# Reuse of the late spill's rows, early loads of the second convolution, and the order of the last sum

## The chip, the cores and the metric

One core of one Trainium2 chip runs one program. The metric is the time of one execution on the device in microseconds (us). TensorE (PE) multiplies, VectorE (DVE) and ScalarE (ACT) compute element by element, GpSimd (POOL) takes a few small operations, and SyncE (SP) issues most of the transfers (DMA) between the core's SBUF and the device's memory.

## The reference

One layer for two groups of tokens with the same weights: 1024 prompt tokens and 256 sample tokens of 1024 features, all in float32. The FFN is 2816 wide.

```python
def short_conv_mixer(x, w_in, conv_w, w_out):
    b, c, v = jnp.split(x @ w_in, 3, axis=-1)
    u = c * v
    up = jnp.pad(u, ((0, 0), (pad, pad), (0, 0)))
    conv = sum(up[:, j:j + S] * conv_w[j] for j in range(CONV_WIDTH))
    return (b * conv) @ w_out
...
def swiglu(x, w_in, w_out):
    gate, up = jnp.split(x @ w_in, 2, axis=-1)
    return (jax.nn.silu(gate) * up) @ w_out
...
        h = rms_norm(x, norms[i, 0])
        x = x + rms_norm(short_conv_mixer(h, ...), norms[i, 1])
        h = rms_norm(x, norms[i, 2])
        x = x + rms_norm(swiglu(h, ffn_w_in[i], ffn_w_out[i]), norms[i, 3])
```

## The kernel before

**Products.** Each float32 operand is split into a high part (rounded by ACT, `copy` L106 or `split` L93) and the rest (DVE, `sub` L97 or `split` L94). Each product is three products of parts (TERMS). Prompt tokens use a form with seven products instead of eight: x1, z5, x6, z3, y2, x7, x4. They add up in three PSUM banks x, y and z. A bank is read out between its products (by ACT's `copy` into `y` in the first group of the output product, by DVE's `add` else), and PE has to wait for that before it writes the bank again.

**Stages.** (1) Input product of the mixer: 12 units (`SEQ`), of which the last makes the last two feature blocks. (2) `store` (L418) splits the gated convolution into `zst` tiles and writes them to memory (`zd`, L424). (3) The second convolution product `mm2` (L664) works by token tile of 128 tokens: it loads `zs` (`load_z`, from `zd`), does 48 products of 128x512 into `mx`, and `after_mm2` makes the norm, the residual x1 and `ht`. `transposes` (L638) turns `ht` round with eight small PE products. `ORDER2` lists the tiles; the first two (0 and 4) run together. (4) FFN in, 22 blocks. (5) FFN out.

**Spill.** The FFN's activations are kept in memory (`actd`). `spill(j)` takes a pair j of feature blocks and makes seven parts of it (`part`). Each part takes a row tile `st{j}_c` of the pools "a" or "s", fills it with one ACT copy and one DVE subtraction, writes it with two stores of 320 KB and returns the row. The next user of the row waits on the chip for those stores to land. The last pair (10) is spilled while the output product is already running, as `st10_0` to `st10_6`; FFN out reads pair 10 in its last group.

**FFN out.** 25 units: five groups of feature pairs times five units of two token tiles (`UNITS`). A unit's data come as one `ut` (1 MB) and three small `us` (256 KB each; for x7, y2 and x4). The weights of pair j come as `w4r{j}` rows and are turned into blocks by ACT and DVE (`weights`). All of it is put in order by a planner that is written out by hand: `clock` holds its estimate of when each engine is free, `slot` (L1119) emits one product, and `advance` (L1067) emits the next background step (a weight step or a spill step) if it would end before a limit. `landing` (L892) is its estimate of when a transfer lands, and `row_free` holds the time from which a row of the pools counts as free. Order on each engine is as emitted, and each engine runs its instructions in order. Unit 4's x4 is emitted two products late, behind the next unit's z5, as for every unit.

**End.** For the last unit (token tiles 8 and 9), `norm_right` and `norm_left` make the squares and the product with the gain for the two halves of a row. `scale` (row, half) then does the last scaling and writes out; half 0 on SP's queue, half 1 on ACT's. `n3r` is the reciprocal root, made by a short DVE step and a power on POOL.

**Pools.** "b" has 23 slots of 8 KB, "a" three rows, "s" two rows.

Of the kernel before, what the change touches and what calls it, by code (L numbers as in the profile page):

```python
# [14 lines left out]
P = 128  # L15
# [21 lines left out]
def encoder_kernel(ctx: ExitStack, tc: tile.TileContext, xT, x, g0T, gB, cwT, w1, w2, w3, w4, out_p, out_s):  # L37
# [51 lines left out]
    def f32(ap):  # L89
        return ap.bitcast(F32)  # L90
# [257 lines left out]
    class EvMul:  # L348
# [69 lines left out]
        def store(self, d):  # L418

            for h in (0, 1):  # L420
                st = get(f"zst{self.e}{d}{h}", [2, HALF], F32R, kind="a")
                split(st[:, 0], st[:, 1], rows[d][:, h])
                for p in (0, 1):
                    nc.sync.dma_start(  # L424
                        zd[h, :, :, p, 2 * self.e + d].rearrange("q p t -> p q t"),
                        f32(st[:, p]).rearrange("p (q t) -> p q t", t=P),
                    )
                put(st)
# [174 lines left out]
    def w2_steps():  # L603
# [5 lines left out]
        while len(w2r) < min(len(w2t) + 3, KD) and (len(free["a"]) > 2 or len(free["b"]) > 2):  # L609
            w2r.append(get(f"w2r{len(w2r)}", [D], kind="a" if len(free["a"]) > 2 else "b"))  # L610
            nc.sync.dma_start(w2r[-1], w2[len(w2r) - 1])

    pending.append(w2_steps)
    for n in range(2, len(SEQ)):
        u = SEQ[n]
        follow = SEQ[n + 1 : n + 3] + [None, None]
        final = n == len(SEQ) - 1
        ev = EvC(u[2]) if u[1] == 1 else EvMul(u[1], u[2])
        if final:
            put(r2)  # L620
            w2_steps()
        b = Block(u, ev, *follow[:2], final)
        b.p12()
        b.p657()
        b.sample()
        b.p43()


# [4 lines left out]
        nc.sync.dma_start(gb[:, i], gB[i].partition_broadcast(P))  # L633
    ar = {(kh, c): get(f"ar{kh}{c}", [KH, 512]) for kh in (0, 1) for c in (0, 1)}
    hs[:] = [get(f"hs{p}", [KD, 256], F32R) for p in "hl"]
    hts, mx, zs = {}, {}, {}

    def transposes(i):  # L638
        for q in range(2):
# [14 lines left out]
                t0 = (i - 8) * P  # L654
                split(*(h[:, 4 * q : 4 * q + 4, t0 : t0 + P] for h in hs), ov)
        put(hts.pop(i))

    def load_z(i, k0=0, k1=KD):
        if i not in zs:
            zs[i] = get(f"zs{i}", [2, KD, P], F32R)  # L660
        src = zd[i // 4, i % 4] if i < 8 else zd[i - 8, 4]
        nc.sync.dma_start(f32(zs[i][:, :, k0:k1]), src[:, :, k0:k1])

    def mm2(*tiles, ks=range(KD)):  # L664
        for i in tiles:
# [27 lines left out]
        nc.vector.scalar_tensor_tensor(out=hts[i], in0=x1, scalar=r, in1=gb[:, 1], op0=ALU.mult, op1=ALU.mult)  # L693
        put(x1)

    ORDER2 = [i for uu in UNITS for i in uu]
    xts = {}

    def load_xt(i):
# [13 lines left out]

    F0, F1, F2 = (("f", f) for f in range(3))
    for i in ORDER2[:2]:
        load_xt(i)
        load_z(i, 0, KD - 2)
    for i in ORDER2[:2]:
        load_z(i, KD - 2, KD)
    for n, i in enumerate(ORDER2):  # L720
        last = n == NT - 1
        if n == 0:
            mm2(i, ORDER2[1])
        elif n > 1:
            if n == 8:
                load_z(ORDER2[9])
                cb["a11"] = [get(f"a11{p}", [KH, 512], F32R) for p in "hl"]
                s3 = get("s3", [KH, 512])
                early_sums(slice(0, 3 * P))
            mm2(i, ks=range(1))  # L730
            transposes(ORDER2[n - 2])
            if last:
                early_sums(slice(3 * P, 4 * P))
            mm2(i, ks=range(1, KH))
            if last:
                put(*w2t[:KH])
                make_c("a12", a12)
                add(a12, a12, a11)
                make(F0, "t24")
                make_c("s2", a11)  # L740
                put(a11)
            mm2(i, ks=range(KH, KD))
        if last:
            put(*w2t[KH:])
        after_mm2(i)
        if n and not last:
            if n != 8:
                load_z(ORDER2[n + 1])
            load_xt(ORDER2[n + 1])
        if n == 4:  # L750
            load(F0)
            for what in ("g", "u", "sums"):
                make(F0, what)
# [11 lines left out]
    def spill(j):  # L765

        a, b = act.pop(2 * j), act.pop(2 * j + 1)
        a11, a21, a12, a22 = a[:, 0], a[:, 1], b[:, 0], b[:, 1]

        def part(c, src, ready=None):  # L770
            done = yield "act", 0.75, ready, 0, 1, 0
            st = get(f"st{j}_{c}", [2, HALF], F32R, kind="as" if j == KP - 1 else "s")
            copy(st[:, 0], src)
            done = yield "dve", 0.76, done, 0, 0, 0
            sub(st[:, 1], src, f32(st[:, 0]))
            for p in range(2):
                nc.sync.dma_start(
                    actd[:, j, :, (2 * c + p) * P : (2 * c + p + 1) * P].rearrange("u p t -> p u t"),
                    f32(st[:, p]).rearrange("p (u t) -> p u t", t=P),
                )  # L780
            put(st)
            return done

        def change(op, out, x, y):
            done = yield "dve", 0.76, None, 0, 0, 0
            op(out, x, y)
            return done

        yield from part(A11, a11)
        yield from part(A12, a12)  # L790
        yield from part(A22, a22)
        done = yield from change(add, a21, a21, a22)
        yield from part(S1, a21, done)
        done = yield from change(sub, a11, a11, a21)
        yield from part(S2, a11, done)
        done = yield from change(add, a22, a22, a11)
        yield from part(S3, a22, done)
        done = yield from change(add, a12, a12, a11)
        yield from part(S4, a12, done)
        put(a, b)  # L800
        act_left.discard(j)
# [265 lines left out]
    def advance(entry, limit):  # L1067
        gen, (engine, cost, ready, places, rows, gi) = entry
        if gi > at["group"] + 1 or places and len(free["b"]) < places + keep() or rows and rows_free() < rows:
            return False  # L1070
        ready = ready() if callable(ready) else ready or 0.0
        if rows:
            tags = (free["s"] + free["a"])[:rows]
            ready = max([ready] + [row_free.get(tag, 0.0) for tag in tags])
        done = max(clock[engine], ready) + cost
        if done > limit:
            return False
        clock[engine] = done
        before = rows_free()
        try:  # L1080
            entry[1] = gen.send(done)
        except StopIteration:
            background.remove(entry)
        if rows_free() > before:
            row_free[(free["a"] + free["s"])[-1]] = done + 4.5
            for tag in free["s"][-1:] + free["a"][-1:]:
                row_free[tag] = max(row_free.get(tag, 0.0), done + 4.5)
        return True

    def fill(limit):  # L1090
# [109 lines left out]
    def norm_left(row):  # L1200
        i = UNITS[-1][row]
        r = tail["r", i]
        squares(tail["acc", i], 0, y_half(row, 0))
        mul(tail["yg", i][:, :H], y_half(row, 0), tail["g3"][:, :H])
        nc.vector.tensor_scalar(
            out=r, in0=tail["acc", i][:, 0:1], scalar1=1.0 / D, scalar2=tail["part", i],
            op0=ALU.mult, op1=ALU.add,
        )
        nc.gpsimd.tensor_tensor(out=r, in0=r, in1=nhalf[:, :1], op=ALU.pow)
# [34 lines left out]
    begin(spill(KP - 1))  # L1244
    with tc.manual_schedule():
        clock.update(pe=0.0, act=1.0, dve=2.0, dma=0.0)
        LAST = len(GROUPS) - 1
        for n, (gi, ui) in enumerate(STREAM):
            at.update(group=gi, unit=n)
            while not set(made).issuperset(GROUPS[gi]):  # L1250
                if not any(advance(entry, 1e12) for entry in list(background)):
                    raise RuntimeError("no place for the weights")
            if gi == LAST:
                load_x1(ui)
            while keep() and len(free["b"]) or rest_asked[0] == 0:
                load_units()
            if first_tiles and first_tiles[0][0] <= n:
                raise RuntimeError("no place for a unit")
            slot(n, "x1")
            slot(n, "z5")  # L1260
            if n:
                slot(n - 1, "x4")
                at["delayed"] = n - 1
                if gi == LAST and ui:
                    begin(finish(ui - 1, 1), 1 if len(background) and background[0][0] is not w4_gen else 0)
            slot(n, "x6")
            slot(n, "z3")
            if n < END:
                slot(n, "y2")
                if gi == LAST:  # L1270
                    begin(finish(ui, 0), 0)
                slot(n, "x7")
        slot(END, "x7")
        while background:
            if not any(advance(entry, 1e12) for entry in list(background)):
                raise RuntimeError("no place at the end")
        norm_right(0)
        norm_right(1)
        slot(END, "y2")
        norm_left(0)  # L1280
        scale(0, 0)
        scale(0, 1)
        slot(END, "x4")
        norm_left(1)
        scale(1, 0)
        scale(1, 1)

# [39 lines left out]
```

## Time and profile before

| what | us |
|---|---|
| median of 3 runs | 1285.08 (1282.38 to 1285.32) |
| the profiled execution | 1286.38 |
| its span, from first to last instruction | 1284.6 |
| PE busy in it | 1246.4 |
| DVE busy | 840.7 |
| ACT busy | 465.4 |

The span is what the trace covers; the 1.78 us beside it lie outside. A row of a timeline gives the start, the length, the engine, the line, the operation with its output and inputs, and the count of equal instructions. A bracket at its end gives the idle time just before it and what ended it.

### The profile page before, as it was taken

Reading aid. Unit: us, or ns where it says so; the run is one execution under the profiler, and the core shown is the slowest. Engines: PE = TensorE matmul, PEld = TensorE weight load, DVE = VectorE, ACT = ScalarE, POOL = GpSimd, SP = SyncE. Lnnn points to the kernel's source line nnn. Section 1 sums busy time; section 2 is a strip of 40 time slices with the busy share of each in tenths; the row PEclk is TensorE's granted clock in tenths of the full one; section 3 lists DMA queues with packets and bytes.
Section 4 is the critical chain, followed back from the end, with each engine's and each line's share of the span. In section 5 each row is a group of like instructions: output and inputs, shape, how many; then the busy total and the mean of one; then the engine's idle time right before and its main releaser. Section 6 shows DMA issues by size and latency. Waiting matters only on the chain.

```text
span 1284.6 us, 15904 instructions
## 1 busy us (share of the span) xinstructions
PE 1246.4 (97%) x6213; PEld 1055.6 (82%) x6213; DVE 840.7 (65%) x1177; ACT 465.4 (36%) x694; POOL 27.0 (2%) x49
## 2 busy tenths in 40 slices
PE   8799999999999989999999999999999979999997
PEld 6588888888778868888888888888888868888885
DVE  7996655748264786565664754755667458769566
ACT  7743333325133553343343333433434331112011
POOL 0100000000011100000000000000000000000000
PEclk9899999999999989999999999999999989999999
DMA  7405041224963213453552643643636789666894
GB/s 263 164 34 148 33 116 66 80 85 147 327 230 115 94 43 118 139 161 100 157 157 87 176 136 97 176 125 95 189 116 213 248 274 329 202 226 212 284 330 167
DMA packets 185595, 207.37 MB, mean 161 GB/s; under 512 B 7984, under 2 KB 145584, under 8 KB 184496
## 3 DMA queue, kind: packets, MB, share of 16 engines
q1 hardware_dynamic: 185088, 205.83, 49.5%
q8 instruction: 49, 0.80, 0.3%
q10 hardware_dynamic: 432, 0.53, 0.1%
q14 instruction: 26, 0.21, 0.1%
HBM read 134.89 MB, written 71.43 MB: 161 GB/s over the span
## 4 chain that ended last, share of the span: by engine, by line
PE 88%; DVE 6%; DMA 3%; ACT 1%; issue 1%; POOL 1%; SPq 0%; DVEq 0%; POOLq 0%; ACTq 0%
PE xo L1131 11%; PE zo L1131 6%; PE mx L672 5%; PE yo L1131 3%; DMA wrf__3029<-w 1%; PE xv__150 L204 1%; PE xf__3543 L204 1%; PE xf__6682 L204 1%; PE xf__3760 L204 1%; PE xf__7635 L204 1%; PE xf__7456 L204 1%; PE xf__7243 L204 1%; PE xf__7069 L204 1%; PE xf__6856 L204 1%; PE xf__6469 L204 1%
## 5 line engine op out<-in xcount | busy, mean ns | idle before, releaser
L672 PE MATMUL mx<-w2s,zs 128*128 128x512 f32 x480 | 111.3, 391 | 3.0 <-DMA zs<-zd 3.0
L672 PEld LDWEIGHTS mx<-w2s,zs 128*128 128x128 f32 x480 | 89.4, 188 | 21.6 <-issue 3.4
L106 ACT ACTIVATE st<-act 128x640 fp32r<-128x640 f32 x77 | 56.8, 737 | 105.2 <-DMA actd<-st 70.0
L97 DVE TENSOR_TENSOR st<-act,st 128x640 fp32r<-128x640 f32 x77 | 63.2, 821 | 28.4 <-ACT st L106 27.7
L100 DVE TENSOR_TENSOR y<-y,xo 128x512 f32<-128x512 f32 x85 | 58.2, 685 | 28.6 <-PE xo L1131 28.3
L1131 PE MATMUL xo<-w4t,us 128*128 128x512 f32 x273 | 68.9, 389 | 0.0
L1131 PE MATMUL xo<-w4t,ut 128*128 128x512 f32 x222 | 57.0, 397 | 6.5 <-ACT y L106 6.5
L1131 PEld LDWEIGHTS xo<-w4t,us 128*128 128x128 f32 x273 | 51.2, 188 | 10.7
L1131 PEld LDWEIGHTS xo<-w4t,ut 128*128 128x128 f32 x222 | 42.3, 191 | 16.0 <-ACT y L106 6.9
L106 ACT ACTIVATE w4t<-w4r 128x1024 fp32r<-128x1024 f32 (+1 forms) x23 | 23.5, 1023 | 73.1 <-DVE w4r L97 60.2
L100 DVE TENSOR_TENSOR y<-y,zo 128x512 f32<-128x512 f32 x45 | 30.8, 685 | 18.2 <-PE zo L1131 17.9
L1131 PE MATMUL zo<-w4b,ut 128*128 128x512 f32 x165 | 42.7, 398 | 0.0
L1131 PE MATMUL xo<-w4b,ut 128*128 128x512 f32 x165 | 41.6, 390 | 0.0
L1131 PE MATMUL zo<-w4t,ut 128*128 128x512 f32 x165 | 41.5, 389 | 0.0
L1163 ACT ACTIVATE junk<-y 128x1024 f32<-128x1024 f32 (+1 forms) x12 | 11.0, 917 | 75.5 <-DVE y L100 74.2
L1131 PEld LDWEIGHTS zo<-w4b,ut 128*128 128x128 f32 x165 | 31.8, 193 | 6.8
L1131 PEld LDWEIGHTS xo<-w4b,ut 128*128 128x128 f32 x165 | 31.0, 188 | 6.6
L1131 PEld LDWEIGHTS zo<-w4t,ut 128*128 128x128 f32 x165 | 31.0, 188 | 6.5
L106 ACT ACTIVATE w4b<-w4r 128x512 fp32r<-128x512 f32 (+1 forms) x22 | 18.0, 838 | 35.1 <-DMA us<-actd 16.0
L414 DVE SCALAR_TENSOR_TENSOR row<-u,cw,row 128x256 f32<-128x256 f32 (+1 forms) x32 | 28.0, 881 | 4.2 <-ACT row L412 3.9
L1131 PE MATMUL yo<-w4b,us 128*128 128x512 f32 x114 | 29.2, 392 | 0.0
L97 DVE TENSOR_TENSOR w4t<-w4r,w4t 128x1024 fp32r<-128x1024 f32 (+1 forms) x23 | 26.9, 1173 | 0.7 <-ACT w4t L106 0.7
(2120 smaller groups left out, 3359.1 us busy)
## 6 DMA issues: line engine op xcount, KB each, us to landing
actd<-st SPq DMA_DIRECT2D x154, 320.0 KB, 2.8
ut<-actd SPq DMA_DIRECT2D x20, 1024.0 KB, 6.6
us<-actd SPq DMA_DIRECT2D x62, 256.0 KB, 4.6
ut<-actd SPq DMA_DIRECT2D x16, 768.0 KB, 8.2
zd<-zst SPq DMA_DIRECT2D x32, 320.0 KB, 3.3
zs<-zd SPq DMA_DIRECT2D x8, 1024.0 KB, 6.7
w4r<-w SPq DMA_DIRECT2D x11, 512.0 KB, 4.0
w4r<-w SPq DMA_DIRECT2D x22, 256.0 KB, 4.5
```

Source lines behind the costliest of these rows:

```text
L97: nc.vector.tensor_tensor(out=out, in0=a, in1=b, op=ALU.subtract)
L100: return nc.vector.tensor_tensor(out=out, in0=a, in1=b, op=ALU.add)
L106: nc.scalar.activation(out, a, AF.Copy)
L204: nc.tensor.matmul(out[:, :n], stat(w, k), mov(part, k), start=first and k == 0 and j == 0, stop=last and k == KH - 1 and j == 2, skip_gro ...
L414: nc.vector.scalar_tensor_tensor(out=out, in0=src, scalar=cw[:, j, dd : dd + 1], in1=out, op0=ALU.mult, op1=ALU.add)
L672: nc.tensor.matmul(mx[i][h], zs[i][:, part, k], w2t[k][:, w, h * H : (h + 1) * H], start=k == 0 and j == 0, stop=k == KD - 1 and j == 2,)
L1131: nc.tensor.matmul(acc, stat[n, c, j][:, ap], w[wp], start=starts and jn == 0 and m == 0, stop=jn == len(grp) - 1 and m == 2, skip_group_c ...
L1163: nc.scalar.activation(junk, src, AF.Square, accum_out=acc[:, col : col + 1])
```

## The change

- `store`: the tiles `zst` of the last feature blocks are taken from pool "b" and no longer from "a".
- `load_z` and `ORDER2` move up. In the last unit of the input product the loads of k 0 to 5 of the first two tiles are issued behind `b.sample()`, ahead of the last two products (`p43`). What is left behind the loop are k 6 and 7.
- `mm2`: for the third and fourth tile six k (36 products) rather than one go ahead of the transposes.
- `part` of `spill`: a returned row counts as free at the planner's estimate of when the part's stores (0.625 MiB) land, plus 1.0. What `advance` noted before (the step's end plus 4.5, for the rows of both pools) goes. `row_free` is emptied at the start of the output product.
- End: `norm_left` becomes a generator that stops ahead of `n3r`. The product x4 of the last unit, with its sum into `y`, is emitted ahead of the scalings of row 0; the squares and the gain of row 1 follow, then one scaling of row 0, `n3r` of row 1, and the other three scalings.

```diff
         def store(self, d):
...
-                st = get(f"zst{self.e}{d}{h}", [2, HALF], F32R, kind="a")
+                st = get(f"zst{self.e}{d}{h}", [2, HALF], F32R, kind="a" if self.e < KH - 1 else "b")
...
         b.sample()
+        if final:
+            for i in ORDER2[:2]:
+                load_z(i, 0, KD - 2)
         b.p43()
...
     for i in ORDER2[:2]:
+        load_z(i, KD - 2, KD)
+    for i in ORDER2[:2]:
         load_xt(i)
-        load_z(i, 0, KD - 2)
-    for i in ORDER2[:2]:
-        load_z(i, KD - 2, KD)
...
-            mm2(i, ks=range(1))
+            early = KD - 2 if n < 4 else 1
+            mm2(i, ks=range(early))
             transposes(ORDER2[n - 2])
             if last:
                 early_sums(slice(3 * P, 4 * P))
-            mm2(i, ks=range(1, KH))
+            mm2(i, ks=range(early, KH))
...
-            mm2(i, ks=range(KH, KD))
+            mm2(i, ks=range(max(early, KH), KD))
...
+            row_free[held[id(st)][1]] = landing(0.625) + 1.0
             put(st)
             return done
...
         clock[engine] = done
-        before = rows_free()
         try:
             entry[1] = gen.send(done)
         except StopIteration:
             background.remove(entry)
-        if rows_free() > before:
-            row_free[(free["a"] + free["s"])[-1]] = done + 4.5
-            for tag in free["s"][-1:] + free["a"][-1:]:
-                row_free[tag] = max(row_free.get(tag, 0.0), done + 4.5)
         return True
...
         mul(tail["yg", i][:, :H], y_half(row, 0), tail["g3"][:, :H])
+        yield
         nc.vector.tensor_scalar(
...
         clock.update(pe=0.0, act=1.0, dve=2.0, dma=0.0)
+        row_free.clear()
...
         slot(END, "y2")
-        norm_left(0)
+        for _ in norm_left(0):
+            pass
+        slot(END, "x4")
+        left = norm_left(1)
+        next(left)
         scale(0, 0)
+        next(left, None)
         scale(0, 1)
-        slot(END, "x4")
-        norm_left(1)
         scale(1, 0)
         scale(1, 1)
```

SP's queue at the end of the input product, before. `zst300` to `zst311` are the tiles of the last two feature blocks, `gb` the gains, `xt` the residual's input.

```order
L633 DMA gb_2578<-gB 128x1024 x2
L424 DMA zd_106<-zst300_2544 128x5x128 x2
L662 DMA zs0_2589<-zd_106 128x2x768
L662 DMA zs4_2593<-zd_106 128x2x768
L424 DMA zd_106<-zst301_2549 128x5x128 x2
L424 DMA zd_106<-zst310_2568 128x5x128 x2
L424 DMA zd_106<-zst311_2573 128x5x128 x2
L701 DMA xt0_2587<-x 128x1024
L701 DMA xt4_2591<-x 128x1024
L662 DMA zs0_2589<-zd_106 128x2x256
L662 DMA zs4_2593<-zd_106 128x2x256
```

The same place now.

```order
L619 DMA zs4_2533<-zd_106 128x2x768
L619 DMA zs0_2531<-zd_106 128x2x768
L645 DMA gb_2582<-gB 128x1024
L424 DMA zd_106<-zst300_2548 128x5x128 x2
L424 DMA zd_106<-zst311_2577 128x5x128 x2
L645 DMA gb_2582<-gB 128x1024
L424 DMA zd_106<-zst301_2553 128x5x128 x2
L706 DMA xt0_2593<-x 128x1024
L424 DMA zd_106<-zst310_2572 128x5x128 x2
L619 DMA zs4_2533<-zd_106 128x2x256
L706 DMA xt4_2595<-x 128x1024
L619 DMA zs0_2531<-zd_106 128x2x256
```

The loads of `zs4` and `zs0` (k 0 to 5) have moved from behind `gb` and two stores to the head of the row; the loads of k 6 and 7 stay behind the stores, and two of the stores have changed places.

ACT in the last units of the first group of the output product, before. `y3` and `y4` are the outputs of units 3 and 4, `xo0_4` and `zo0_4` unit 4's banks.

```order
L106 ACTIVATE st10_1_8029<-act20_7455 128x640
L106 ACTIVATE y3_8065<-xo0_3_8056 128x512
L106 ACTIVATE y3_8065<-zo0_3_8067 128x512
L106 ACTIVATE st10_2_8081<-act20_7455 128x640
L106 ACTIVATE y2_7977<-xo0_2_7967 128x512
L106 ACTIVATE w4b11_1_7935<-w4r3_8025 128x512
L106 ACTIVATE y3_8065<-xo0_3_8056 128x512
L106 ACTIVATE w4b22_3_8108<-w4r3_8025 128x1024
L106 ACTIVATE st10_5_8139<-act21_7634 128x640
L106 ACTIVATE y4_8141<-xo0_4_8129 128x512
L106 ACTIVATE w4t13_3_8150<-w4r3_8025 128x1024
L106 ACTIVATE y4_8141<-zo0_4_8143 128x512
```

The same place now.

```order
L106 ACTIVATE y3_8059<-xo0_3_8050 128x512
L106 ACTIVATE st10_1_8068<-act20_7455 128x640
L106 ACTIVATE y3_8059<-zo0_3_8061 128x512
L106 ACTIVATE y2_7972<-xo0_2_7962 128x512
L106 ACTIVATE w4b11_1_7930<-w4r3_8019 128x512
L106 ACTIVATE y3_8059<-xo0_3_8050 128x512
L106 ACTIVATE w4b22_3_8110<-w4r3_8019 128x1024
L106 ACTIVATE y4_8132<-xo0_4_8122 128x512
L106 ACTIVATE y4_8132<-zo0_4_8134 128x512
L106 ACTIVATE w4t13_3_8149<-w4r3_8019 128x1024
L106 ACTIVATE y3_8059<-xo0_3_8050 128x512
L106 ACTIVATE y4_8132<-xo0_4_8122 128x512
```

`st10_2` and `st10_5` no longer stand among these rows: `st10_1` is the one spill copy left there, and behind `w4b22_3` come both first copies of unit 4 directly.

SP's queue at the same place, before. `ut5` and `us4` are the loads of units 5 and 4.

```order
L923 DMA w4r40_8042<-w4 128x1024
L925 DMA w4r41_8043<-w4 128x512 x2
L1007 DMA ut5_0_8063<-actd_108 128x2x1024
L1007 DMA us4_4_0_8090<-actd_108 128x2x256
L1007 DMA us4_5_0_8092<-actd_108 128x2x256
L1007 DMA us4_6_0_8094<-actd_108 128x2x256
L777 DMA actd_108<-st10_2_8081 128x5x128 x2
L1007 DMA ut6_0_8136<-actd_108 128x2x1024
L777 DMA actd_108<-st10_5_8139 128x5x128 x2
```

The same place now.

```order
L929 DMA w4r40_8036<-w4 128x1024
L931 DMA w4r41_8037<-w4 128x512 x2
L1013 DMA ut5_0_8057<-actd_108 128x2x1024
L782 DMA actd_108<-st10_1_8068 128x5x128 x2
L1013 DMA us4_4_0_8088<-actd_108 128x2x256
L1013 DMA us4_5_0_8090<-actd_108 128x2x256
L1013 DMA us4_6_0_8092<-actd_108 128x2x256
L1013 DMA ut6_0_8129<-actd_108 128x2x1024
L1013 DMA us5_4_2_8160<-actd_108 128x2x256
L1013 DMA us5_5_2_8162<-actd_108 128x2x256
L1013 DMA us5_6_2_8164<-actd_108 128x2x256
L782 DMA actd_108<-st10_2_8185 128x5x128 x2
```

Two stores (`st10_1`) stand ahead of the three `us4` where before two (`st10_2`) stood behind them, and `us5` follows `ut6` directly.

DVE at the end, before. `xo4_4` is the bank of the last product x4; rows 8 and 9 are the last unit's two token tiles.

```order
L100 TENSOR_TENSOR y4_8141<-y4_8141,yo4_4_9748 128x512
L103 TENSOR_TENSOR yg8_9735<-y4_8141,g3_9252 128x512
L1205 TENSOR_SCALAR n3r8_9733<-n3e8_9732,n3p8_9734 128x1
L1214 SCALAR_TENSOR_TENSOR y4_8141<-yg8_9735,n3r8_9733,x1l4_9655 128x512 x2
L100 TENSOR_TENSOR y4_8141<-y4_8141,xo4_4_9658 128x512
L103 TENSOR_TENSOR yg9_9743<-y4_8141,g3_9252 128x512
L1205 TENSOR_SCALAR n3r9_9741<-n3e9_9740,n3p9_9742 128x1
L1214 SCALAR_TENSOR_TENSOR y4_8141<-yg9_9743,n3r9_9741,x1l4_9655 128x512 x2
```

The same place now.

```order
L100 TENSOR_TENSOR y4_8132<-y4_8132,yo4_4_9747 128x512
L103 TENSOR_TENSOR yg8_9734<-y4_8132,g3_9251 128x512
L1207 TENSOR_SCALAR n3r8_9732<-n3e8_9731,n3p8_9733 128x1
L100 TENSOR_TENSOR y4_8132<-y4_8132,xo4_4_9657 128x512
L103 TENSOR_TENSOR yg9_9742<-y4_8132,g3_9251 128x512
L1216 SCALAR_TENSOR_TENSOR y4_8132<-yg8_9734,n3r8_9732,x1l4_9654 128x512
L1207 TENSOR_SCALAR n3r9_9740<-n3e9_9739,n3p9_9741 128x1
L1216 SCALAR_TENSOR_TENSOR y4_8132<-yg8_9734,n3r8_9732,x1l4_9654 128x512
L1216 SCALAR_TENSOR_TENSOR y4_8132<-yg9_9742,n3r9_9740,x1l4_9654 128x512 x2
```

The sum that takes `xo4_4` has moved ahead of both scalings of row 8, and `n3r9` ahead of the second of them.

## Rows read from the trace of the kernel before

**Rows 1.** Page, part 1: engine, busy us (share of the span), instructions.

```profile
PE 1246.4 (97%) x6213; PEld 1055.6 (82%) x6213; DVE 840.7 (65%) x1177; ACT 465.4 (36%) x694; POOL 27.0 (2%) x49
```

**Rows 2.** PE's waits, whole span: us in total, times, longest.

```profile
PE xo L1131 <- ACT y L106: 6.5, 1, 6.5
...
PE mx L672 <- DMA zs<-zd: 3.0, 1, 3.0
```

**Rows 3.** PE's timeline, end of the output product's first group.

```profile
1041.41 1.52 PE L1131 MATMUL zo<-w4t,ut 128*128 128x512 f32 x6
1042.77 1.52 PE L1131 MATMUL xo<-w4t,us 128*128 128x512 f32 x6
1050.79 2.93 PE L1131 MATMUL xo<-w4t,ut 128*128 128x512 f32 x6 [6.50 <-ACT y L106]
1053.51 2.76 PE L1131 MATMUL zo<-w4b,ut 128*128 128x512 f32 x6
1056.07 1.78 PE L1131 MATMUL yo<-w4b,us 128*128 128x512 f32 x6
1057.69 1.52 PE L1131 MATMUL xo<-w4t,us 128*128 128x512 f32 x6
```

**Rows 4.** PE's timeline, from the input product to the second convolution.

```profile
324.53 0.39 PE L204 MATMUL zp__2372<-s4h,wup__2222 128*128 128x512 f32 x1
327.88 28.37 PE L672 MATMUL mx<-w2s,zs 128*128 128x512 f32 x124 [2.96 <-DMA zs<-zd]
357.43 1.09 PE L642 MATMUL tr<-ident,ht 128*128 128x128 f32 x8 [1.17 <-DVE ht L693]
...
367.74 1.06 PE L642 MATMUL tr<-ident,ht 128*128 128x128 f32 x8 [0.77 <-DVE n_1t L132]
```

**Rows 5.** SP's timeline of the same stretch: issues of transfers.

```profile
313.73 0.80 SPq L633 DMA_DIRECT2D gb<-gB  x2
...
321.91 1.37 SPq L662 DMA_DIRECT2D zs<-zd  x2
```

**Rows 6.** DMA issues (KB each, us to landing): whole span, at 1038.1, at 1039.65.

```profile
actd<-st SPq DMA_DIRECT2D x154, 320.0 KB, 2.8
...
us<-actd SPq DMA_DIRECT2D x1, 256.0 KB, 8.0
...
actd<-st SPq DMA_DIRECT2D x1, 320.0 KB, 8.8
```

**Rows 7.** ACT's timeline in the stretch of rows 3.

```profile
1049.51 0.74 ACT L106 ACTIVATE st<-act 128x640 fp32r<-128x640 f32 x1 [11.80 <-DMA actd<-st]
```

**Rows 8.** Windows: us; PE, PEld, DVE, ACT, POOL busy; PEclk, DMA share, GB/s.

```profile
1036.00:1040.00 4.00, 4.00 (x19) 3.34 (x18) 3.27 (x6) 1.55 (x2) 0.00 (x0) 1.00 0.70 221
1046.00:1048.00 2.00, 0.00 (x0) 0.00 (x0) 0.00 (x0) 0.00 (x0) 0.00 (x0) 0.59 1.13 345
1052.00:1054.00 2.00, 2.00 (x7) 1.52 (x6) 1.34 (x2) 1.85 (x4) 0.00 (x0) 0.50 0.98 249
...
1062.00:1088.00 26.00, 26.00 (x116) 21.55 (x115) 23.39 (x34) 6.32 (x7) 0.00 (x0) 1.00 0.96 340
```

**Rows 9.** SP's timeline in the stretch of rows 3.

```profile
1038.12 1.50 SPq L1007 DMA_DIRECT2D us<-actd  x3
1039.67 2.45 SPq L777 DMA_DIRECT2D actd<-st  x2
```

**Rows 10.** PE's timeline, the last products.

```profile
1272.93 2.21 PE L1131 MATMUL xo<-w4t,us 128*128 128x512 f32 x9
```

**Rows 11.** DVE's timeline at the end.

```profile
1275.67 1.41 DVE L1214 SCALAR_TENSOR_TENSOR y<-yg,n3r,x1l 128x512 f32<-128x512 f32 x2 [0.65 <-POOL n3r L1209]
1277.00 0.68 DVE L100 TENSOR_TENSOR y<-y,xo 128x512 f32<-128x512 f32 x1
...
1279.47 1.42 DVE L1214 SCALAR_TENSOR_TENSOR y<-yg,n3r,x1l 128x512 f32<-128x512 f32 x2 [0.72 <-POOL n3r L1209]
```

More of the change, by code (lines that the diff above doesn't have):

```diff
@@ L611, in w2_steps, with load_z @@
             nc.sync.dma_start(w2r[-1], w2[len(w2r) - 1])
+    zs = {}
+    def load_z(i, k0=0, k1=KD):
+        if i not in zs:
+            zs[i] = get(f"zs{i}", [2, KD, P], F32R)
+        src = zd[i // 4, i % 4] if i < 8 else zd[i - 8, 4]
+        nc.sync.dma_start(f32(zs[i][:, :, k0:k1]), src[:, :, k0:k1])
+    ORDER2 = [i for uu in UNITS for i in uu]
     pending.append(w2_steps)
@@ L635, in encoder_kernel @@
     hs[:] = [get(f"hs{p}", [KD, 256], F32R) for p in "hl"]
-    hts, mx, zs = {}, {}, {}
+    hts, mx = {}, {}
     def transposes(i):
@@ L656, in transposes @@
         put(hts.pop(i))
[L658 to L662, printed above, removed]
     def mm2(*tiles, ks=range(KD)):
@@ L694, in after_mm2 @@
         put(x1)
-    ORDER2 = [i for uu in UNITS for i in uu]
     xts = {}
```

## The prediction

> **What bounds the kernel now.** The page's first part comes first: TensorE (PE) is busy for 97% of the span and no other engine is near it [rows 1]. An edit can pay only where PE stands still or runs at the lower clock, so the second view is the list of what PE waited for. Two entries of it lie where the change works: 6.5 us once for a copy by ScalarE (ACT) in the output product, and 3.0 us once for the load of `zs` [rows 2]. The PE timelines of those two stretches and of the end follow. The unit of account is the pitch of a 128x512 product: groups of six start 1.36 us apart (1041.41, 1042.77 [rows 3]), so 0.227 us for one. All of this is one profiled execution of 1286.38 us with a span of 1284.6. The median of the three timed runs is 1285.08 (1282.38 to 1285.32), 1.3 below it: what a stretch loses is read from the profiled execution, and the sum is then taken off both.
>
> **Part A, from the first convolution to the second.** The last product of the first starts at 324.53, the next would be due at 324.76, and the first `mx` starts at 327.88: 3.12 us are lost, and the row says to a DMA, `zs<-zd` [rows 4]. The SP timeline shows why: those loads were issued at 321.91, behind stores, while SP had been free to issue (`gb`) at 313.73 [rows 5]. The change puts both loads just ahead of `gb`, so at about 313.7, 11 us before they are needed. The late issue took 6.0 us from 321.91 to 327.88; the slowest landing that I read elsewhere is 8.8 [rows 6]. So the 3.12 go whole. What could hold the loads is a slot of the pool "b"; the tiles that free the two slots are read for the last time at around the issue of `gb`, which is why I place them there.
>
> The same stretch has two waits of the transposes for `ht`: 1.17 and 0.77 us [rows 4]. The PE order moves tile 0's transposes from behind 124 products to behind 132, tile 4's from 161 to 180. Tile 0's last product is the 90th, 90 x 0.227 = 20.4 after 327.88, at 348.3; `ht` came at 357.43, 9.1 later. Now it comes at 324.76 + 20.4 + 9.1 = 354.3, and PE reaches the transposes at 324.76 + 132 x 0.227 = 354.7. The first wait goes, by 0.4. For tile 4 the extra 19 products are 4.3 us against 0.77. The next in line are the remaining `zs` loads (k 6 and 7), needed when 72 of the 96 first products are through, 16 us after 324.76; they still follow the last block's stores in SP's queue, with 1.5 MB fewer ahead of them, so I put no wait there. Sum of A: 3.1 + 1.2 + 0.8 = 5.1, of which I take **5.0** for the thin margin. Bounds: 0, if the loads find no slot before the stores, and 5.1.
>
> **Part B, the late spill.** Unit 3's last group starts at 1042.77, so the next (bank `xo`, unit 4) is due at 1044.13. It starts at 1050.79 after 6.50 us of waiting for ACT [rows 3]. ACT itself was blocked for 11.80 us in the copy `st<-act`, for the landing of earlier stores `actd<-st`; the copy `y<-xo`, which empties PE's bank, stands right behind it [rows 7]. The order names it: `st10_5` ahead of `y4<-xo0_4`. After the stall the three groups 1050.79, 1053.51 and 1056.07 run at a pitch of 2.7, 2.6 and 1.6, with a granted clock of 0.50, the 1.2 GHz level [rows 3, 8]. The fourth starts at 1057.69, and was due at 1044.13 + 3 x 1.36 = 1048.21. Thus **9.48 us** in all: 6.66 of wait and 2.8 of low clock.
>
> Before, a row that a spill had left counted as free at a time that did not know how full the transfers were: the store that blocked took 8.8 us to land, and the median of its kind is 2.8 [rows 6]. Now the row counts as free by the planner's own sum of transfers. In the order ACT's next two copies of unit 4 follow `w4b22_3` at once, and `st10_2`, `st10_5`, `st10_3` come one by one, far later. So nothing stands before `y4<-xo0_4` but a weight copy that was done long before 1044 in the old order too: the wait on ACT goes, and with it the low clock.
>
> What is late next is a load. Before, SP issued the three `us` of unit 4 at 1038.12 and the two stores of `st10_2` behind them; the first `us` landed 8.0 later, at 1046.1 [rows 6, 9]. Now the two stores of `st10_1` stand ahead of them. Those are 655 KB; at 345 GB/s, the rate of 1046 to 1048 with the transfers at their full share [rows 8], 1.9 us. So the first `us` lands at 1048.0. Its product y2 was hidden behind the stall until now; it is due at 1044.13 + 2 x 1.36 = 1046.85. New wait: 1.2 us. Bounds: zero, if the store overlaps, and 2.5: the two stores hold SP for up to 2.45 (the row of 1039.67 [rows 9]), so issue at 1040.57, and with the 8.8 of a store 1049.4. I take 1.2, since transfers and not SP are full there. The 3.12 us of part A's stall is near in length to this wait and was followed by products at normal pitch (28.37 us for 124 [rows 4]), so no low clock is charged. B is 9.5 - 1.2 = **8.3**, bounds 0 and 9.5.
>
> The Trainium skill ("DMA: Bandwidth & Descriptors", section "Queues, rings and completion order") speaks against this move: descriptors of one DMA engine are taken in ring order, and the increment of the semaphore lands only after earlier writes of that engine, so a load that is queued behind stores is reported done only after the stores are written. By it the wait is at least the stores' 8.8 us from about 1039.1, to 1047.9, so 1.1 us; by free overlap it would be none. The landings here came in order of issue (1046.1 for the `us`, 1039.67 + 8.8 = 1048.5 for a store behind it), which agrees with the page without proving it.
>
> The spill's later end moves traffic. `ut8`, `st10_5`, three `us7`, the 1 MB loads of `w4r5`, `w4r6`, `w4r7`, `st10_3`, `ut9` and the first `us8` stand in SP's queue ahead of unit 8's y2. That is 7.25 MiB, 7.6 MB, between about 1062 and 1046.85 + 1.2 + 4 x 42 x 0.227 = 1086.2. It needs 314 GB/s; 1062 to 1088 moved 340 on the mean [rows 8]. I charge nothing, with little to spare.
>
> **Part C, the end.** The last products start at 1272.93 and end 2.21 later, at 1275.14 [rows 10]. The sum that takes them (`y<-y,xo`) starts at 1277.00, because two scalings of 0.7 us each are ahead of it on VectorE (DVE), the first waiting 0.65 for GpSimd; the last pair of scalings starts at 1279.47, after 0.72 of the same [rows 11]. Now the sum starts at 1275.2 and its product with g3 follows (0.7 each, to 1276.6). One scaling of row 0 covers the time to 1277.2, `n3r` of row 1 (some 0.2) follows at once and then 0.72 for GpSimd as before. The last row's scalings can start at 1278.1 in place of 1279.47: 1.3. Four output stores of 256 KB now come closer together on two queues; no row shows that. It costs between nothing and one store's 0.76 us (262 KB at the 345 GB/s above); I take 0.3, nearer to nothing, since no loads are left beside them. C is **1.0**, bounds 0.5 and 1.3.
>
> **Edits at nothing.** `zst` in "b" slots rather than "a": ACT and SP wait less, PE does not follow them there. `gb` later: it is used first in `after_mm2`, behind 20 us of products; were it later than that, its lateness would be added to `ht`'s wait. `row_free.clear()` and the removed bookkeeping issue no instruction. `w4r5` later: unit 10 is the first to need its blocks, six units of 9.5 us after 1044.13, at 1101, and its load moves behind some two units' loads of a queue that no longer stalls; without that cover PE waits for weights there, the slower rival below.
>
> **Sum.** 5.0 + 8.3 + 1.0 = 14.3. 1286.38 - 14.3 = 1272.1 for a profiled execution, and 1285.08 - 14.3 = **1270.8** for the median. 0.3% (3.9 us) is about what a measurement of this kernel can tell from no change.
>
> **Rivals.**
> - *No new wait* (0.12): the stores overlap with the loads and y2 finds its `us`. B is 9.5: 1269.6. For it: the share of the DMA engines at 1036 to 1040 is 0.70 [rows 8], so there is room; against it, the landings in order.
> - *Two larger waits* (0.16): 2.5 at unit 4's y2 and 2.5 at unit 8's, from the traffic above. B is 4.5: 1274.6.
> - *The stall only moves* (0.08): the new spill order blocks ACT or the queue elsewhere, as some stores still land in 8.8, and PE loses 9.5 in another group. B is 0: 1279.1, with half of its weight beyond 1281.2, which is the bound of no change. Against it: `st10_2`'s copy now stands behind all the early copies of unit 4.
> - *Slower* (0.04): one mechanism. `w4r61` reuses the row of `st10_3` and waits in SP's queue for its landing; ten loads are behind it. If the 7.6 MB then move at under 192 GB/s, they end 39.6 us after 1062, 15.4 past 1086.2; with 2.8 of low clock that is 18.2, more than the 14.3 by the 3.9. At 190: 1289.4. Against it: the lowest rate read beside such a wait of SP is 221 [rows 8].
>
> The forecast itself has 0.60. Faster by over 0.3%: 0.60 + 0.12 + 0.16 and half of 0.08, 0.92; within: 0.04; slower: 0.04. The range takes in the first three cases (0.88): from 1267.5, the no-wait case less the 2 us by which single runs differ, to 1278.5, two waits of 2.5 with the low clock once and A's second half (1.2) missing.
>
> **What would show it.** A: `mx` starts 0.2 us after the last `zp`, no wait of `tr` for `ht`. B: no `xo` waiting for ACT, granted clock 1.00 there, and in its place about 1.2 for `us` at unit 4's y2. C: the sum of `xo` starts within 0.2 of the last product's end. It would be wrong if the list of PE's waits has a new entry above 3 us between unit 4 and unit 10, or a slice at half clock there.

## The result and the profile after

The changed kernel takes 1275.78 us in the median of 14 runs (1271.61 to 1282.06), the kernel before 1284.85 (14 runs, 1281.78 to 1286.99): a ratio of 0.9933, 95% interval 0.9918 to 0.9947. That is 9.1 us between the medians where 14.3 were forecast. The profiled execution of the changed kernel took 1271.61 us (span 1269.8), the fastest of its 14. So it shows the mechanisms, and not the median.

The page, part 1 of the changed kernel, answers to [rows 1]:

```profile
PE 1242.1 (98%) x6213; PEld 1052.6 (83%) x6213; DVE 841.0 (66%) x1177; ACT 466.4 (37%) x694; POOL 26.5 (2%) x49
```

PE's waits answer to [rows 2] (us in total, times, longest). The waits for `y` by ACT and for `zs` are gone; a wait for `us` is new, and it comes twice.

```profile
PE yo L1132 <- DMA us<-actd: 2.4, 2, 1.3
...
PE tr L654 <- DVE ht L699: 0.3, 1, 0.3
```

PE's timeline at the transition, against [rows 4]: `mx` follows the last `zp` by the usual 0.23, and the first two groups of transposes (L654) wait for nothing.

```profile
323.30 0.39 PE L204 MATMUL zp__2372<-s4h,wup__2222 128*128 128x512 f32 x1
323.53 30.08 PE L678 MATMUL mx<-w2s,zs 128*128 128x512 f32 x132
353.49 1.09 PE L654 MATMUL tr<-ident,ht 128*128 128x128 f32 x8
...
365.34 1.04 PE L654 MATMUL tr<-ident,ht 128*128 128x128 f32 x8
```

PE's timeline in the output product, against [rows 3]: x6 of unit 4 (1036.83) starts at the usual pitch. The y2 of units 4 and 8 (`yo<-w4b,us`) wait.

```profile
1035.47 1.52 PE L1132 MATMUL xo<-w4t,us 128*128 128x512 f32 x6
1036.83 1.52 PE L1132 MATMUL xo<-w4t,ut 128*128 128x512 f32 x6
1038.19 1.52 PE L1132 MATMUL zo<-w4b,ut 128*128 128x512 f32 x6
1040.87 1.66 PE L1132 MATMUL yo<-w4b,us 128*128 128x512 f32 x6 [1.16 <-DMA us<-actd]
...
1080.53 1.66 PE L1132 MATMUL yo<-w4b,us 128*128 128x512 f32 x6 [1.26 <-DMA us<-actd]
```

The end, PE's timeline and then DVE's, against [rows 10, 11]: the sum that takes the last products starts at 1261.43, 0.04 after they end (1259.19 + 2.20), where it stood 1.86 behind them before. The last scalings start 3.33 after the products' end, before 4.33.

```profile
1259.19 2.20 PE L1132 MATMUL xo<-w4t,us 128*128 128x512 f32 x9
```

```profile
1261.43 0.69 DVE L100 TENSOR_TENSOR y<-y,xo 128x512 f32<-128x512 f32 x1
...
1264.72 1.42 DVE L1216 SCALAR_TENSOR_TENSOR y<-yg,n3r,x1l 128x512 f32<-128x512 f32 x2 [0.44 <-POOL n3r L1211]
```

**Stage by stage.** All these kernels run 6213 PE products. Each length below is the difference of two starts in PE's timelines, by the number of the product in PE's order; the first row counts from the span's start, the last from the start of the very last product. Stretches that aren't shown differ by under 0.4 us between any two traces. `same` and `same2` are further executions of the changed kernel, `no_spill` and `both` are experiments that follow.

| stretch (product numbers) | before | changed | same | same2 | no_spill | both |
|---|---|---|---|---|---|---|
| the span's start to the first prompt product (250) | 71.03 | 69.80 | 71.51 | 70.76 | 70.19 | 70.12 |
| last `zp` to first `mx` (1593 to 1594) | 3.35 | 0.23 | 0.23 | 0.23 | 0.23 | 0.23 |
| second convolution (1594 to 1900) | 68.22 | 66.31 | 66.33 | 66.31 | 66.29 | 67.10 |
| start of FFN in (2138 to 2400) | 56.21 | 55.36 | 55.35 | 55.34 | 55.33 | 56.25 |
| FFN out to x1 of unit 5 (5058 to 5262) | 55.93 | 47.71 | 48.11 | 47.80 | 55.56 | 46.24 |
| to y2 of unit 8 (5262 to 5418) | 35.36 | 36.78 | 37.33 | 37.30 | 35.36 | 35.36 |
| to the fifth group (5418 to 5700) | 63.92 | 64.06 | 65.68 | 65.69 | 63.92 | 63.92 |
| start of the last product (6212) to the span's end | 9.85 | 8.82 | 8.83 | 8.83 | 8.85 | 8.86 |

In the first pair of traces A gives 3.12 + 1.91 = 5.03, B 8.22 - 1.42 - 0.14 = 6.66, C 1.03: 12.7. The other 2.1 of the 14.8 between the spans stand at the start and at the start of FFN in. The start moves by as much between executions of one kernel (69.80, 71.51, 70.76), and the start of FFN in takes 54.9 to 56.5 over all the traces, with part A and without it (it is shortest, 54.9, in `no_tail` and `w4_waits`, the two traces whose granted clock stays at 1.00 there); neither is claimed for the change.

The table says where the median went too. Measured against `both`, which waits for no load, the three stretches of FFN out lose 9.69 us in the kernel before, 3.03 in the first trace of the changed one, and 5.60 and 5.27 in `same` and `same2`.

### The profile page after: what moved, and what is told of

Same layout as the page of the kernel before. It is cut to its first block, busy times and chain, and to the rows that moved or that the text cites. A ratio compares the mean times of both kernels' runs of the same rounds, so it can differ in the third digit from the quotient of the medians.

```text
span 1269.8 us, 15906 instructions
## 1 busy us (share of the span) xinstructions
PE 1242.1 (98%) x6213; PEld 1052.6 (83%) x6213; DVE 841.0 (66%) x1177; ACT 466.4 (37%) x694; POOL 26.5 (2%) x49
## 4 chain that ended last, share of the span: by engine, by line
PE 88%; DVE 5%; DMA 3%; issue 1%; ACT 1%; POOL 1%; SPq 1%; POOLq 0%; DVEq 0%; ACTq 0%
PE xo L1132 11%; PE zo L1132 5%; PE mx L678 4%; PE yo L1132 3%; DMA us<-actd 1%; PE xf__6682 L204 1%; PE xf__3760 L204 1%; PE xp__710 L204 1%; PE xf__7635 L204 1%; PE xf__7456 L204 1%; PE xf__7243 L204 1%; PE xf__7069 L204 1%; PE xf__6856 L204 1%; PE xf__5521 L204 1%; PE xf__5308 L204 1%
```

## The experiments

**First set: the changed kernel again, and each part undone.** The theory was that executions of the changed kernel lose the missing 4 us behind the new waits for `us`; the rival, that they lose them where the change does nothing.

> The changed kernel again, to read a second execution of it. Its profiled execution took 1271.6 and its median 1275.8, so most executions lose some 4 us somewhere. Theory: they lose it behind the two new waits for us (1.16 and 1.26 us in the first profile), where the clock falls in some executions: then the granted clock below 1.00 between 1040 and 1100, median 1275 to 1276. Rival: they lose it at places that the change does not touch (the first 80 us, the start of FFN in near 455): then the clock is 1.00 from 470 on, in an execution of over 1274 too.

It took 1275.7 us (6 runs, 1272.14 to 1278.80; ratio 0.9934, 0.9917 to 0.9951), its profiled execution 1275.83. Both are partly right. The start is 1.7 longer than in the first trace. The waits are 1.57 and 1.80, and behind the second the clock falls. PE's timeline of `same`:

```profile
1042.92 1.66 PE L1132 MATMUL yo<-w4b,us 128*128 128x512 f32 x6 [1.57 <-DMA us<-actd]
...
1083.11 1.93 PE L1132 MATMUL yo<-w4b,us 128*128 128x512 f32 x6 [1.80 <-DMA us<-actd]
1084.83 2.76 PE L1132 MATMUL xo<-w4t,us 128*128 128x512 f32 x6
1087.39 1.72 PE L1132 MATMUL xo<-w4b,ut 128*128 128x512 f32 x6
```

The same place in windows (us; PE, PEld, DVE, ACT, POOL busy; PEclk, DMA share, GB/s): twelve products in 4 us in place of 19, at a mean granted clock of 0.57.

```profile
1084.00:1088.00 4.00, 4.00 (x12) 3.12 (x11) 1.06 (x2) 0.00 (x0) 0.00 (x0) 0.57 1.05 378
1088.00:1092.00 4.00, 4.00 (x19) 3.29 (x18) 1.82 (x4) 1.06 (x1) 0.00 (x0) 1.00 0.96 353
```

The low clock costs 65.68 - 63.92 = 1.76 there, on top of the wait.

`no_spill`, the old bookkeeping of rows:

```diff
-            row_free[held[id(st)][1]] = landing(0.625) + 1.0
...
+        before = rows_free()
...
+        if rows_free() > before:
+            row_free[(free["a"] + free["s"])[-1]] = done + 4.5
+            for tag in free["s"][-1:] + free["a"][-1:]:
+                row_free[tag] = max(row_free.get(tag, 0.0), done + 4.5)
...
-        row_free.clear()
```

> The changed kernel with the old bookkeeping of row_free (part B undone, A and C kept). By the prediction B is worth 8.3: 1284.1 where the changed kernel has 1275.8. Rival: the stall of 9.5 of the first profile is a long one, and the median of B is about 4: 1280. Rival to the naming of the cause: with other tags free after part A the old rule may place the spill without that stall, then about 1276.

1279.1 us (6 runs, 1277.21 to 1279.99; 0.9960, 0.9945 to 0.9974): 3.4 above `same`, not 8.3. But the stall is all there, 6.56 us on PE and 11.87 on ACT, with the clock low behind it (groups at a pitch of 2.73 and 2.37). PE's timeline and ACT's:

```profile
1044.10 2.93 PE L1136 MATMUL xo<-w4t,ut 128*128 128x512 f32 x6 [6.56 <-ACT y L106]
1046.83 2.54 PE L1136 MATMUL zo<-w4b,ut 128*128 128x512 f32 x6
1049.20 1.55 PE L1136 MATMUL yo<-w4b,us 128*128 128x512 f32 x6
```

```profile
1042.83 0.74 ACT L106 ACTIVATE st<-act 128x640 fp32r<-128x640 f32 x1 [11.87 <-DMA actd<-st]
```

Its price is 55.56 - 46.24 = 9.32, as the 9.48 of the prediction. So the bookkeeping is what places the stall, and tags freed by part A don't help. What the change takes away is as large as forecast; what it puts in its place is larger.

`no_transition`, part A undone:

```diff
-                st = get(f"zst{self.e}{d}{h}", [2, HALF], F32R, kind="a" if self.e < KH - 1 else "b")
+                st = get(f"zst{self.e}{d}{h}", [2, HALF], F32R, kind="a")
...
-                load_z(i, 0, KD - 2)
         b.p43()
...
     for i in ORDER2[:2]:
         load_xt(i)
+        load_z(i, 0, KD - 2)
...
-            early = KD - 2 if n < 4 else 1
+            early = 1
```

> The changed kernel without its part A: zst from pool a, the first zs loads behind the loop, one k ahead of the transposes. By the prediction A is worth 5.0: PE waits 3.1 for zs and 1.9 for ht again, so 5.0 above the changed kernel's median of the same call (1280.8 if that is 1275.8). If other executions lose part of it anyway, the difference is 3 or less.

1277.83 us (6 runs, 1274.14 to 1280.31; 0.9948, 0.9930 to 0.9965), 2.1 above `same` in the medians, not 5.0. Its trace has the waits of before again: 3.20 to the first `mx` and 68.21 for the second convolution, 4.9 more than `same`. With executions of either kernel 6 us apart the medians don't decide between 2 and 5; a later pair does.

`no_tail`, part C undone:

```diff
+        scale(0, 0)
+        scale(0, 1)
         slot(END, "x4")
-        left = norm_left(1)
-        next(left)
-        scale(0, 0)
-        next(left, None)
-        scale(0, 1)
+        for _ in norm_left(1):
+            pass
```

> The changed kernel with the old end (part C undone). By the prediction 1.0 slower than the changed kernel, bounds 0.5 and 1.3; in the trace the time from the end of the last product to the end of the span is 9.5 (as before) in place of 8.4.

1274.77 us (6 runs, 1270.34 to 1276.86; 0.9923, 0.9905 to 0.9940): below `same` where 1.0 above was expected, inside what these runs can tell. The trace is clear: from the last product's start to the span's end 9.86, against 8.82. It shows something else as well: the y2 of unit 4 starts at the usual pitch here, though nothing of B was undone, and only unit 8 waits (1.21).

**Second set: which cause the waits for `us` have.** SP's timeline of the changed kernel shows two candidates. The stores of `st10_1` (1030.93) stand ahead of unit 4's three `us` (1031.97). And SP stands still ahead of both units' loads: `w4r41` is issued 6 us after `w4r40` (1023.52, 1029.54), `w4r61` 6.6 after `w4r60` (1062.95, 1069.54).

```profile
1023.52 1.17 SPq L929 DMA_DIRECT2D w4r<-w  x1
1029.54 0.82 SPq L931 DMA_DIRECT2D w4r<-w  x2
1030.40 0.43 SPq L1013 DMA_DIRECT2D ut<-actd  x1
1030.93 0.98 SPq L782 DMA_DIRECT2D actd<-st  x2
1031.97 4.96 SPq L1013 DMA_DIRECT2D us<-actd  x3
...
1062.95 1.20 SPq L929 DMA_DIRECT2D w4r<-w  x1
1069.54 0.82 SPq L931 DMA_DIRECT2D w4r<-w  x2
...
1072.31 1.67 SPq L1013 DMA_DIRECT2D us<-actd  x3
```

SP's waits from 1015 to 1085 (us in total, times, longest) name what it stood for there (L931 is the second row of a weight load): the landing of stores that had been issued just ahead. It stood longer in all for DVE's half of the spill's rows, the first entry of the list; that wait is also in `w4_waits` below, where PE waits for nothing (10.5, 4, 5.2).

```profile
SPq L782 <- DVE st L97: 12.0, 4, 5.2
SPq L931 <- DMA actd<-st: 10.1, 2, 5.3
```

`us_early` takes the stores out of the way, `w4_waits` the standing still, `both` does both:

```diff
+        if name == "x4":
+            at["delayed"] = n
         fill(ready + 0.5)
```

```diff
+    def rows_landed(n):
+        return all(row_free.get(tag, 0.0) <= clock["pe"] for tag in (free["s"] + free["a"])[:n])
...
-        elif rows_free() >= 2 + bool(act_left):
+        elif rows_free() >= 2 + bool(act_left) and rows_landed(2):
```

> The changed kernel, with each unit's three us issued one product sooner, so that unit 4's stand ahead of the two stores of st10_1. If those stores are what makes unit 4 wait (as the prediction has it), its 1.2 us go and unit 8's 1.3 stay, where no such store stands ahead: from x6 of unit 4 to y2 of unit 8 42.3 us in place of 43.7. If SP's blocked queue is the cause (it stands 5 to 6 us at w4r41, ahead of both), the wait stays about 1 us.

1271.34 us (5 runs, 1270.52 to 1273.55; 0.9909, 0.9894 to 0.9924). Unit 4 no longer waits (5.44 from its x6 to x1 of unit 5, the bare pitch of 24 products). Unit 8 still does, for 2.49: SP stands at `w4r61` as before, and all that stood ahead of unit 8's `us` still does. From x6 of unit 4 to y2 of unit 8 it took 5.44 + 38.01 = 43.5, not 42.3; that miss is unit 8's longer wait. PE's timeline:

```profile
1082.37 1.66 PE L1132 MATMUL yo<-w4b,us 128*128 128x512 f32 x6 [2.49 <-DMA us<-actd]
```

> The changed kernel, with a load of w4 rows planned only when both rows count as landed (row_free), so that SP does not stand at w4r41 and w4r61 for the landing of a store just issued. If those blocked 5 to 6 us of SP are the cause, both waits for us go, no half clock is left between 1030 and 1100 in any execution, and the four stretches from x6 of unit 4 to the end of group 3 take 40.8 less: the median is 3 to 5 below the changed kernel's. Rival: transfers as such are full; then the waits stay at 1 us or come back at unit 10 for the weights.

1270.45 us (5 runs, 1269.34 to 1272.37; 0.9902, 0.9887 to 0.9917), 3.9 below `same2`. Neither unit waits, with the stores of `st10_1` still ahead of unit 4's `us`. Here the y2 of units 4 and 8 start one pitch of 1.36 behind the products ahead of them. PE's timeline of `w4_waits`:

```profile
1040.40 1.52 PE L1135 MATMUL zo<-w4b,ut 128*128 128x512 f32 x6
1041.76 1.52 PE L1135 MATMUL yo<-w4b,us 128*128 128x512 f32 x6
...
1078.48 1.52 PE L1135 MATMUL zo<-w4b,ut 128*128 128x512 f32 x6
1079.84 1.52 PE L1135 MATMUL yo<-w4b,us 128*128 128x512 f32 x6
```

So at unit 4 either edit is enough: the stores make it wait only together with what delays SP's queue ahead of them. At unit 8 `w4_waits` is enough. But it does more than take the standing away: a load that isn't planned yet also leaves its place in the queue. SP's timeline of `w4_waits` has `w4r4` at 1044.01, behind the `us` of units 4 and 5, and `w4r7` at 1081.89, behind those of unit 8; in the changed kernel they are issued at 1023.52 and 1070.42, ahead of them. (In the kernel before, `w4r4` stood ahead too, `w4r7` behind, at 1082.78.)

```profile
1044.01 0.82 SPq L932 DMA_DIRECT2D w4r<-w  x1
...
1081.89 0.34 SPq L932 DMA_DIRECT2D w4r<-w  x1
```

So 1 MB less stands ahead of each of the two loads, some 3 us at the 330 GB/s below (an estimate), which alone is longer than any wait for `us` here. No run takes away the standing and keeps the order, so which of the two it is stays open. What the traces do show is the rate. Windows of the changed kernel and of `w4_waits`, the 26 us up to the y2 of unit 8 (the columns as above):

```profile
1054.00:1080.00 26.00, 25.26 (x112) 20.60 (x110) 22.19 (x33) 4.56 (x5) 0.00 (x0) 1.00 0.86 273
1054.00:1080.00 26.00, 26.00 (x116) 21.55 (x115) 22.83 (x33) 5.62 (x6) 0.00 (x0) 1.00 0.92 330
```

The rival that transfers as such are full does not fit the first row: the DMA engines were idle for part of these 26 us. (The "40.8 less" of the expectation is a slip: 40.8 is the length of the stretch up to x6 of unit 4, not a gain.)

> Both edits. By either cause neither wait is left: the time from the first output product to the start of y2 of unit 8 is 81.6 us where the changed kernel has 84.5, and the median 3 to 5 below it, 1271 to 1273. If the medians' gap to the first profile came from places that the change does not touch, the median falls by no more than 2.

1269.87 us (5 runs, 1268.76 to 1271.01; 0.9895, 0.9879 to 0.9911), a little below the 1271 to 1273 expected, with 81.60 from the first output product to the y2 of unit 8, as expected. The third execution of the changed kernel, beside it:

> The changed kernel a third time, beside the three above on the same chip. Median 1275 to 1276. Both waits for us again, 1.1 to 1.8 each; where one is 1.8 or longer the clock is 0.50 for a time behind it, as in the second execution (1.8 at unit 8), and 1.00 behind the shorter ones.

1274.34 us (6 runs, 1271.25 to 1278.88; 0.9933, 0.9915 to 0.9950), just under the 1275 expected, with waits of 1.24 and 1.78 and the clock low behind the second. So without the waits for `us` the median falls by 4.5, and the distance between the fastest and the slowest run falls from 7.6 to 2.3. So these waits, with the low clock behind them, are what the changed kernel's executions lose most by. Against its first profile the theory has the larger share and the rival the rest: of the 4.2 and 3.3 us by which the spans of `same` and `same2` are longer, 2.6 and 2.2 lie in FFN out and 1.7 and 1.0 at the start. The part on the clock held for these traces and fails on others: `us_early` waited 2.49 and `only_spill`, below, 1.88, both with the clock at 1.00 behind it. A wait's length alone does not tell whether the clock falls.

**Third set: A, C and B on steadier ground.** With `both` as the base, A and C are undone by the diffs above.

> Both edits again, as the base of the two beside it: without waits for us its executions differ little, so the worth of A and C can be read from medians. Median 1269 to 1271, all executions within 3 us.

1270.54 us (4 runs, 1269.79 to 1271.08; 0.9898, 0.9884 to 0.9912).

> Both edits, with part A undone. If A is worth what its stage shows (3.1 for zs, 1.9 for ht), the median is 5 above the base; where ht comes late in the base too (a split of the first FFN weight stands ahead of it on DVE, and its load lands at different times), 3 to 5. If the 2.1 between the medians of the first comparison were the whole worth, 2.

1274.48 us (6 runs, 1272.27 to 1277.72; 0.9933, 0.9918 to 0.9948): 3.9 above the base, with no run in common. The traces say why it is not 5.0. Without A the wait for `zs` isn't always 3 us; here PE's timeline has 1.08:

```profile
325.50 28.39 PE L677 MATMUL mx<-w2s,zs 128*128 128x512 f32 x124 [1.08 <-DMA zs<-zd]
355.06 1.09 PE L653 MATMUL tr<-ident,ht 128*128 128x128 f32 x8 [1.17 <-DVE ht L698]
365.37 1.06 PE L653 MATMUL tr<-ident,ht 128*128 128x128 f32 x8 [0.77 <-DVE n_1t L132]
```

And with A the transposes of tile 0 wait in some executions: nothing in the first trace, 0.95 in `both2`, 2.56 in `w4_waits`, whose code is the same up to there. In `w4_waits` DVE's split of the first FFN weight, which stands ahead of `ht` on DVE, starts at 352.08, behind ACT's half of it (2.87 of idle); in the first trace it started at 349.13. PE's timeline and DVE's of `w4_waits`:

```profile
356.17 1.09 PE L654 MATMUL tr<-ident,ht 128*128 128x128 f32 x8 [2.56 <-DVE ht L699]
```

```profile
352.08 1.23 DVE L94 TENSOR_TENSOR wgf__3032<-wrf__3029,wgf__3032 128x1024 fp32r<-128x1024 f32 x1 [2.87 <-ACT wgf__3032 L93]
```

ACT's half was late because the weight's load landed late, though the row does not name it. The load was issued at 335.65 in the first trace and at 337.21 in `w4_waits`; the DMA issues of the two, in this order (KB, us to landing), put its landing at 347.3 and 350.9.

```profile
wrf__3029<-w SPq DMA_DIRECT2D x1, 512.0 KB, 11.7
wrf__3029<-w SPq DMA_DIRECT2D x1, 512.0 KB, 13.7
```

ACT's half starts at 347.39 and 350.98, within 0.1 of the landing, and so it does in the other traces with part A. Why the load lands at such different times stays open: SP's order of transfers is the same in all of them up to there.

> Both edits, with part C undone: 1.0 above the base, in every execution; the last stage 9.85 in place of 8.85.

1270.90 us (4 runs, 1270.42 to 1273.17; 0.9905, 0.9890 to 0.9920): 0.4 above the base in the medians, which is inside the spread of the runs. In the trace the last stage is 9.82 against 8.83 in `both2`: 0.99.

> The kernel before with part B alone (A and C undone). The stall of ACT and its low clock go (from x6 of unit 4 to the end of group 3 9.7 us of loss before), the two waits for us come, 3 to 5.6 with the low clock behind them: 4 to 6.5 below the kernel before.

1278.89 us (12 runs, 1276.82 to 1287.93; 0.9973, 0.9956 to 0.9989; the kernel before beside it 1282.67): 3.8 below the kernel before, just under what was expected. Its trace has the two waits for `us`, 1.88 and 1.58, the clock at 1.00 behind both, and no stall of ACT.

## Why the prediction was right or wrong

**The range and the direction held**: 1275.78 lies in 1267.5 to 1278.5, and faster it is. **The predicted time, 1270.8, is 5.0 too low**, and B is where most of it went.

- *A, 5.0.* Right in its steps: 5.03 in the first pair of traces, the `zs` wait and both waits of the transposes gone. As a median on the steadier base it is 3.9. I took one execution's wait of 3.12 for all of them (3.12, 2.97, 1.24 and 0.92 above the pitch in four traces of kernels without A). And I kept only 0.1 for a margin that I put at 0.4; in the first trace it is 0.06 (DVE writes `ht` from 352.15 to 353.43, the transposes start at 353.49), and in other executions it is overrun by up to 2.6.
- *B, what it removes, 9.5.* Right: 9.69 in the trace of before against `both`, 9.32 in `no_spill`.
- *B, what it adds, 1.2.* The wait at unit 4 was right in place, and at 1.16 in size in the first trace; the stores are a part of its cause and not the whole (`us_early`, `w4_waits`). **The step that failed is the budget for unit 8**: 7.6 MB at 314 GB/s needed, 340 moved, so "I charge nothing". The list of transfers was right, and the rate was not: 340 was read in the kernel before, where `w4r61` is issued 2.7 us behind `w4r60` (1069.27, 1071.98). In the changed kernel it is 6.6, and the 26 us up to the y2 of unit 8 move 273 GB/s, less than the 314 needed. I had named SP's wait at `w4r61` in the rival "slower", and gave it a price only at a rate of under 192 GB/s; y2 of unit 8 waits 1.0 to 2.5 in the seven traces that have B and not `w4_waits`. In six of them (without `us_early`) the new waits with the low clock cost 1.6 (`no_tail`) to 5.6, so that B is worth 9.7 less that, 4.1 to 8.1; the two comparisons of medians give 3.4 and 3.8, below that, and why is open: no second execution of the kernel before was traced. The nearest rival is "two larger waits", 1274.6 us, which I gave 0.16; its loss is about right, its sizes are not, since part of the loss is low clock.
- *No low clock behind the new wait.* Argued from the 2.96 us wait for `zs`, after which the clock stayed at 1.00. It holds in the first trace and not in `same` and `same2`, where 1.8 us at unit 8 cost 1.8 more. That is the slice at half clock by which the prediction wanted to be called wrong; its other sign, a wait above 3 us, came in no trace with B.
- *C, 1.0.* Right: 1.03 and 0.99 in traces. The medians can't show it.
- *The page of the Trainium skill.* Of "DMA: Bandwidth & Descriptors", section "Queues, rings and completion order", I took that a load queued behind stores counts as done only after them. The trace agrees, without proving it: the second store of `st10_1`, issued at about 1031.4, landed 8.7 later, at 1040.1, and the first `us`, issued at 1031.97, 8.9 later, at 1040.8. DMA issues of the changed kernel from 1031.9 to 1032.3 (KB, us to landing):

```profile
actd<-st SPq DMA_DIRECT2D x1, 320.0 KB, 8.7
us<-actd SPq DMA_DIRECT2D x1, 256.0 KB, 8.9
```

So the worked median should have been 1285.08 - (3.9 + 3.6 + 1.0) = 1276.6, from what the runs gave: A as found on the base, C as its traces have it, B as the mean of its two medians.

`both` is faster than either kernel: 1269.87 and 1270.54 us, 0.9895 (0.9879 to 0.9911) and 0.9898 (0.9884 to 0.9912) of the time before.

## What to carry to other kernels

When a stall of 9.5 us goes, look for the loads that it used to cover, and follow each through its issuing queue. A rate read in the old order does not carry over to the new one: here 340 GB/s became 273 in a stretch where SP's queue stood longer. A planner's rule that a row is free when its store has landed has to hold for every user of the row; here the spill got it, and the weight loads that take the same rows kept SP's queue standing until they got it too. An experiment that plans a transfer later moves its place in the queue as well, so it does not show by itself which of the two helped. And a profiled execution is one draw: terms read from waits on transfers need the wait of several executions, while terms on an engine's own order (C, the pitch) come back to 0.05 us.

## What the runs showed of the hardware that was not expected

Between executions of one kernel nearly every stretch of PE repeats to 0.1 us; what differs are the waits on transfers and the clock behind them. Short waits do not settle the clock by their length: 1.78 and 1.80 us were followed by a stretch of the 1.2 GHz level (granted clock 0.50, pitch 2.56 for six products in place of 1.36), and 1.88, 2.49, 2.56 and 2.96 us were not.
